# Prompt attention of a latent-attention layer: fifth score product with 128 rows, one rotary product for two heads, latent queries split after their norm

## Chip, core, metric

The kernel runs on one core of a Trainium2 chip (trn2). The metric is device time in microseconds of the whole program, on that core. A core has a tensor engine (PE, with PEld for its weight loads), a vector engine (DVE), a scalar engine (ACT), GpSimd (POOL) and SyncE (SP), which here only issues transfers; each takes its own instructions in order and they wait for each other by semaphores.

## What is computed

One step of a two-layer decoder trunk on 1024 prompt tokens and 8 sample tokens (1032 columns): a gated linear recurrence with its feed-forward block, then multi-head latent attention (MLA) with another. The change lies in the prompt's part of MLA. There are 8 heads, latents of 256 features, rotary keys of 64, queries from 384 latent features:

```python
q = (rmsnorm(h @ w_dq, q_a_norm) @ w_uq).reshape(B, T, H_B, NOPE + ROPE_DIM)   # 128 + 64
q_nope, q_rope = q[..., :NOPE], rope(q[..., NOPE:], pos)
...
s = (jnp.einsum('bthc,bsc->bhts', ql, c_all)
     + jnp.einsum('bthr,bsr->bhts', qr, kr_all)).astype(jnp.float32) * SCALE
s = jnp.where(k_pos <= q_pos, s, MASK_VALUE)
p = jax.nn.softmax(s, axis=-1)
return jnp.einsum('bhts,bsc->bthc', p, c_all)
...
def rope(x, pos):    # halves of 32
    return jnp.concatenate([x1 * cos - x2 * sin, x2 * cos + x1 * sin], axis=-1)
```

For the prompt the kernel expands the keys and values of each head from the latents instead of absorbing the projection into the query.

## The kernel before, in words

Everything is kept transposed, features on the partitions and the 1032 tokens in the free dimension, cut in NS = 3 spans of W = 344. A float32 value x is held as two parts, hi (rounded to the tensor engine's one-pass float32 format, F32R) and lo = x - hi; `split` (lines 127 to 130) makes them, hi on ACT and lo on DVE or another engine, and `mm3` (lines 172 to 179) forms a product as three: hi hi, hi lo, lo hi.

**Entry of MLA**, `mla_in` (lines 1137 to 1240). Six 128-column products with x give the latents (`cf`), the rotary keys (`krt`) and the latent queries (`qa`, three chunks of 128). `keys(s)` normalises the latents of a span and rotates the keys: the rotary columns are projected twice, straight and with their halves swapped (`swapped`, line 1079), so that one product with the table `tab` and one addition give the rotation. The key goes to `krs` (its hi part, on rows 0 to 63 and again on 64 to 127) and `krl` (its lo part, 64 rows). `queries(s)` splits `qa` of a span at once, then forms its norm; since the split queries are not normalised, the factor is kept in `rqs` and, times the table, in `rtab`.

**Prompt attention**, `mla_prompt`. `prep(h)` is a generator that projects one head in steps: two for its keys (`kh`, `kl`), then for each span one step for the 128 plain query columns (product, times `rqs`, split: hi on ACT, lo on POOL) and one for the rotary ones (128 columns: 64 straight and 64 swapped; times `rtab` on DVE, a copy of the lower half on ACT, an addition, then hi on rows 0 to 63 and lo on rows 64 to 127 of `qrs`). An even head also makes the values of itself and the next head, four steps. So a head has 8 steps, an even one 12.

`scores(h, i)` takes 128 queries (row block i of 8) against the keys up to them, in pieces of 256 to 512 columns (`PIECES`, 12 pieces for the 8 row blocks). A piece is a sum of five products in one PSUM bank:

```python
nc.tensor.matmul(out, lhsT=qrs[:, ts], rhs=krs[:, ks], start=False, stop=False)         # line 1341
last = n == len(pcs) - 1
nc.tensor.matmul(out, lhsT=qrs[0:ROPE, ts], rhs=krl[:, ks], start=False, stop=not last)  # line 1343
```

Lines 1338 to 1340 are the three of the latent part, 1341 is (hi, lo) against the hi keys with 128 rows, 1343 hi against the lo keys with 64 rows. The last piece of a row block gets the causal mask by a bfloat16 product (line 1346). Then DVE takes the maximum (1347), ACT the exponentials (1356), DVE scales (1361). `turn` transposes the weights on PE (1377) two row blocks later (LAG), `pv` multiplies with the values.

**Order.** `attend()` yields after each row block of each head; the loop at its end emits, after row block i of head h, the steps of `prep(h + 1)` that are due: `n = 8 + (4 if (h + 1) % 2 == 0 else 0)` spread over the 8 row blocks. After head 7 the place of `prep` is taken by the first work of the sample tokens (`sample_first`). From these the framework builds the order of each engine with a model of its own, `schedule_with_timeline_sim=True`; PSUM tiles come from a ring of 8 banks.

Of the kernel before, what the change touches and what calls it, by code (L numbers as in the profile page):

```python
# [8 lines left out]
F32 = mybir.dt.float32  # L9
F32R = mybir.dt.float32r  # L10
# [27 lines left out]
class Core:  # L38
    """Pools, constants and the pieces that every sub-layer shares."""
# [37 lines left out]
    def first_x(self, x_prompt):  # L77
        """Loads the first span of the input, in tiles of 128 tokens, a tile a step."""
# [28 lines left out]
    def load_gains(self, rows, among):  # L107
        """rows: (AP [n, 128]) list, transposed into one column per row. among: other loads' steps."""
# [18 lines left out]
    def split(self, hi, lo, src, lo_eng=None):  # L127
        """src = hi + lo exactly, both in the one-pass format."""
# [3 lines left out]
    def weight(self, src, a, b, gain=None, pool=None, nb=2, place=None, eng=None):  # L132
        """Loads [128, a, b] of a weight, times gain[:, a], as hi and lo parts."""
# [38 lines left out]
    def mm3(self, out, terms, first=True, last=True):  # L172
        """Sum of stationary^T moving over terms of ((wh, wl), (ah, al))."""
# [10 lines left out]
    def xproduct(self, wt, s, n=None):  # L184
        """A weight's product with a span of x; n: its number among the next sub-layer's first weights."""
# [27 lines left out]
    def put_x(self, s, c, y, gain):  # L213
        """x[s] chunk c = y * gain, as hi and lo parts."""
# [13 lines left out]
class Squares:  # L228
    """Sum of the squares of the KC chunks of a span. Four chunks at a time are summed over their
    partitions in the four column groups of the tensor engine."""  # L230
# [5 lines left out]
    def add(self, src, eng=None, place=None):  # L236
        """src: the next chunks of the span."""
# [27 lines left out]
def result(gen):  # L265
    """Runs a generator to its end; what it returns."""
# [7 lines left out]
# Order in which steps of neighbouring parts are emitted, for each sub-layer and part.  # L274
# [252 lines left out]
def ffn_first(w_in):  # L527
    """The first weights that ffn asks for."""
# [4 lines left out]
def ffn(k, w_in, w_out, r, end):  # L533
    nc, tc = k.nc, k.tc
    w_in = w_in.rearrange("(c p) f -> p c f", p=P)
    with ExitStack() as st:
# [6 lines left out]
        def inp(f):  # L543
            """The gated products of 128 of the features, a span a step."""
# [55 lines left out]
class OutProj:  # L600
    """acc[s] = w_out^T o, with o read back from DRAM into the tiles of x, which get the new x of a
    span when its products are done. The first span goes head by head, as weights arrive."""
# [16 lines left out]
    def first(self, n, heads=H - 1):  # L619
        """The first n heads' part of the first span, kept in the place of the last span."""  # L620
# [74 lines left out]
class HgrnGates:  # L695
    """Per-feature constants of the forget gate from the lower bounds, one column per head."""
# [30 lines left out]
def hgrn(k, c, w_in, gnorm, lbl, state, load, st_p, st_s, o_dram, v_dram, out):  # L727
    """Gated recurrence, one head at a time, in chunks of 128 tokens.

    Scores inside a chunk are split by the largest power of two that separates the two tokens:  # L730
    for each, both sides are scaled by their decay to a token between them, so that no exponent
    is positive. Distances from 32 up fill their own blocks of A; the shorter ones stay in the
    four 32-token blocks on the diagonal and are picked by a mask."""
# [7 lines left out]
    with ExitStack() as st:  # L741
# [22 lines left out]
        def proj(h):  # L764
            """Projections of one head, one span of one of them a step: f, q, i, g."""
# [89 lines left out]
        def gate(h, sig):  # L855
            """gnorm * g * sigmoid(g), in place of g."""
# [233 lines left out]
def swapped(src, lo):  # L1090
    """Sources of 64 rotary columns followed by the same with their halves swapped."""
# [810 lines left out]
```

## Time and profile before

| | us |
|---|---|
| device time, three runs | 3000.06, 3000.13, 2996.25; median 3000.06 |
| span of the profiled execution, first to last instruction | 2994.8 |
| PE busy | 2848.2 (95%) |
| DVE busy | 1787.6 (60%) |
| ACT busy | 1084.2 (36%) |
| POOL busy | 1014.8 (34%) |
| last work chain, share of the span by engine | PE 75%, DVE 15%, ACT 4%, issue 4%, POOL 1%, DMA 1% |
| MLA's entry | about 1560 to 1645 |
| prompt attention | 1645 to 1955 |
| sample attention, later half | 1955 to 2107 |

The time of the profiled execution itself is given by its span alone; the lowest of the three runs is 1.5 us above it and the median 5.3 us. Times of the trace count from the start of the span. A matmul's row has its start and a modelled end; matmuls overlap, so what one costs is read from start to start. "Idle before" and an arrow name what an engine waited for; L1343 is line 1343.

### The profile page before, as it was taken

The numbers are of one execution on the slowest core, as the hardware profiler recorded it, in microseconds if no ns is written. First come the engines' busy times: TensorE is split into PE (matmuls) and PEld (weight loads), VectorE is DVE, ScalarE is ACT, GpSimd is POOL, SyncE is SP. The second block draws the span as 40 slices with busy tenths as digits, with TensorE's granted clock in tenths as the row PEclk, the third lists the DMA queues.
The fourth block names the chain that finished last, engine by engine and source line by source line (L and its number), as shares of the span: only waits on it lengthen the run. The fifth ranks groups of instructions, "written<-read, shape, count | busy, mean of one in ns | idle before, by whom it ended". The sixth has DMA issues, their size and how long they took to land.

```text
span 2994.8 us, 54870 instructions
## 1 busy us (share of the span) xinstructions
PE 2848.2 (95%) x22468; PEld 2648.1 (88%) x22468; DVE 1787.6 (60%) x3526; ACT 1084.2 (36%) x2216; POOL 1014.8 (34%) x936
## 2 busy tenths in 40 slices
PE   7899889899999999999999999978999999999998
PEld 7888888888899999999878888845879999999998
DVE  8888888873444454444377777786353445444445
ACT  6555555555511111111255555533443111111112
POOL 3455455453422333223241111253134233322330
PEclk9999999999999999999999999989999999999999
DMA  5122222153311111111141111477432111111112
GB/s 180 52 65 64 66 63 63 59 190 100 116 50 43 48 48 48 49 43 50 29 128 51 39 47 50 143 294 272 135 105 66 43 49 48 48 49 43 50 47 103
DMA packets 237084, 242.26 MB, mean 81 GB/s; under 512 B 25443, under 2 KB 217489, under 8 KB 230817
## 3 DMA queue, kind: packets, MB, share of 16 engines
q1 hardware_dynamic: 211568, 169.87, 18.8%
q0 software_dynamic: 7456, 43.00, 3.9%
q10 hardware_dynamic: 17808, 25.89, 2.4%
q8 instruction: 177, 2.90, 0.4%
q14 instruction: 75, 0.61, 0.1%
HBM read 194.60 MB, written 44.12 MB: 80 GB/s over the span
## 4 chain that ended last, share of the span: by engine, by line
PE 75%; DVE 15%; ACT 4%; issue 4%; POOL 1%; DMA 1%; DVEq 0%; ACTq 0%; SPq 0%; POOLq 0%
PE ps L177 22%; PE ps L178 21%; PE ps L179 21%; PE ps L1450 2%; PE ps L252 2%; DVE X L878 1%; DVE E L875 1%; PE ps L1343 1%; DVE E L874 1%; PE ps L1377 1%; PE ps L1338 1%; DVE qe L927 1%; ACT sig L830 1%; DVE b L826 1%; DVE turned L1450 1%
## 5 line engine op out<-in xcount | busy, mean ns | idle before, releaser
L177 PE MATMUL ps<-xh,w 128*128 128x344 f32 x3360 | 1106.8, 330 | 1.7 <-ACT xh L221 1.7
L178 PE MATMUL ps<-xl,w 128*128 128x344 f32 x3360 | 1086.3, 323 | 1.7 <-DVE xl L222 1.7
L179 PE MATMUL ps<-xh,w 128*128 128x344 f32 x3360 | 1081.6, 322 | 0.0
L155 POOL TENSOR_TENSOR w<-raw,w 128x512 fp32r<-128x512 f32 (+1 forms) x360 | 468.1, 1321 | 794.4 <-ACT w L151 773.3
L177 PEld LDWEIGHTS ps<-xh,w 128*128 128x128 f32 x3360 | 641.3, 191 | 24.5 <-issue 10.9
L178 PEld LDWEIGHTS ps<-xl,w 128*128 128x128 f32 x3360 | 640.7, 191 | 15.3 <-issue 8.8
L179 PEld LDWEIGHTS ps<-xh,w 128*128 128x128 f32 x3360 | 640.1, 191 | 6.0 <-issue 5.6
L582 DVE TENSOR_TENSOR acc<-ps,acc 128x344 f32<-128x344 f32 x864 | 397.6, 514 | 0.0
L151 ACT CAST w<-raw 128x1024 fp32r<-128x1024 f32 (+3 forms) x206 | 207.6, 1008 | 423.8 <-PE ps L179 322.6
L177 PE MATMUL ps<-gh,w 128*128 128x344 f32 x1056 | 339.5, 323 | 0.5 <-ACT gh L129 0.3
L179 PE MATMUL ps<-gh,w 128*128 128x344 f32 x1056 | 339.1, 321 | 0.0
L178 PE MATMUL ps<-gl,w 128*128 128x344 f32 x1056 | 338.7, 321 | 0.0
L557 POOL TENSOR_TENSOR u<-u,a 128x344 f32<-128x344 f32 x132 | 122.2, 927 | 533.1 <-DVE u L556 528.5
L556 DVE TENSOR_TENSOR u<-ps,r 128x344 f32<-128x344 f32 x132 | 68.1, 516 | 388.6 <-PE ps L179 388.3
L129 ACT CAST gh<-u 128x344 fp32r<-128x344 f32 x132 | 63.5, 481 | 503.9 <-POOL u L557 503.9
L552 DVE TENSOR_TENSOR a<-ps,r 128x344 f32<-128x344 f32 x132 | 68.1, 516 | 233.1 <-PE ps L179 227.0
L177 PEld LDWEIGHTS ps<-gh,w 128*128 128x128 f32 x1056 | 198.7, 189 | 5.3 <-issue 1.7
L178 PEld LDWEIGHTS ps<-gl,w 128*128 128x128 f32 x1056 | 199.2, 189 | 1.1 <-DVE gl L130 0.8
L179 PEld LDWEIGHTS ps<-gh,w 128*128 128x128 f32 x1056 | 199.1, 189 | 1.1 <-issue 1.1
L130 DVE TENSOR_TENSOR gl<-u,gh 128x344 fp32r<-128x344 f32 x132 | 70.1, 531 | 150.5 <-ACT gh L129 150.5
L553 ACT ACTIVATE a<-a 128x344 f32<-128x344 f32 x132 | 64.5, 490 | 224.0 <-DVE a L552 223.8
L877 POOL TENSOR_TENSOR X<-lin,E 128x256 f32<-128x256 f32 x112 | 108.8, 976 | 79.2 <-ACT E L876 50.4
(373 smaller groups left out, 4178.6 us busy)
## 6 DMA issues: line engine op xcount, KB each, us to landing
raw<-in_w_ffn_in_dram SPq DMA_DIRECT2D x88, 512.0 KB
raw<-in_w_ffn_out_dram SPq DMA_DIRECT2D x44, 512.0 KB
raw<-in_w_in_a_dram SPq DMA_DIRECT2D x32, 512.0 KB
xs<-x_d SPq DMA_DIRECT2D x72, 172.0 KB
x_d<-acc ACTq DMA_DIRECT2D x9, 1376.0 KB
x_d<-y SPq DMA_DIRECT2D x3, 1376.0 KB
od_a<-oh ACTq DMA_DIRECT2D x24, 172.0 KB
od_a<-ol ACTq DMA_DIRECT2D x24, 172.0 KB
```

The source lines that it names most:

```text
L130: (lo_eng or self.nc.vector).tensor_tensor(out=lo, in0=src, in1=hi, op=ALU.subtract)
L151: nc.scalar.copy(wh[:, :n], raw[:, :n])
L155: eng.tensor_tensor(out=wl[:, sl], in0=raw[:, sl], in1=wh[:, sl], op=ALU.subtract)
L177: nc.tensor.matmul(out, lhsT=wh, rhs=ah, start=first and i == 0, stop=False)
L178: nc.tensor.matmul(out, lhsT=wh, rhs=al, start=False, stop=False)
L179: nc.tensor.matmul(out, lhsT=wl, rhs=ah, start=False, stop=last and i == n - 1)
L552: nc.vector.tensor_tensor(out=a, in0=pg, in1=r[s], op=ALU.mult)
L556: nc.vector.tensor_tensor(out=u, in0=pu, in1=r[s], op=ALU.mult)
L557: nc.gpsimd.tensor_tensor(out=u, in0=u, in1=a, op=ALU.mult)
L582: nc.vector.tensor_tensor(out=acc[s][:, dc, :], in0=po, in1=acc[s][:, dc, :], op=ALU.add)
L877: nc.gpsimd.tensor_tensor(out=Xl[:, :, 0, :], in0=kl[:, :, 0, :], in1=El[:, :, 0, :], op=ALU.mult)
L1450: return lambda *a, **kw: self.tc.keep_in_program_order(getattr(self.eng, name)(*a, **kw))
```

## The change

- `krl` gets 128 rows, the lo key twice, and the fifth product takes all 128 rows of `qrs`: hi and lo against the lo keys.
- An even head's `prep` projects the plain rotary columns of itself and the next head side by side (64 + 64 columns). The rotation takes the swapped halves by four copies of 32 rows on ACT out of PSUM (`sw`), two products with full tables `rcos` and `rsin`, an addition, and two splits of 64 rows. An odd head has no rotary product. The odd head's rotary query (`qr1`) has lo on top and hi below, two buffers. An odd head has 5 steps, an even one 12.
- `queries(s)` forms the norm first, multiplies `qa` by it and by SCALE, and splits after that; so the plain query needs no factor: hi and lo straight from PSUM, lo on DVE.
- `rqs` and `rtab` are gone; `rcos` and `rsin`, same size, are loaded by two more transfers of 128 x 1032 on SP. Small tiles move to `k.rp` (tags r0, r1).

The diff, without docstrings and the renaming of arguments:

```diff
-            krs, krl = krp[:, 0], krp[0:ROPE, 1]
+            krs, krl = krp[:, 0], krp[:, 1]
-            rqs = qp.tile([P, T], F32, name="rqs")
-            rtab = qp.tile([P, T], F32, name="rtab")
+            rcos, rsin = (qp.tile([P, T], F32, name=n) for n in ("rcos", "rsin"))
...
-        nc.sync.dma_start(out=tab, in_=c["rope"])
+        for n, t in enumerate((tab, rcos, rsin)):
+            nc.sync.dma_start(out=t, in_=c["rope"][n])
...
-            nc.scalar.copy(kr[:, sl], krt[ROPE:P, sl])
-            nc.vector.tensor_tensor(out=kr[:, sl], in0=kr[:, sl], in1=krt[0:ROPE, sl], op=ALU.add)
+            kt = ip.tile([ROPE, W], F32, name="kt", tag="nat", bufs=2)
+            nc.scalar.copy(kt, krt[ROPE:P, sl])
+            nc.vector.tensor_tensor(out=kr[:, sl], in0=kr[:, sl], in1=kt, op=ALU.add)
...
-            nc.vector.tensor_tensor(out=krl[:, sl], in0=kr[:, sl], in1=krs[0:ROPE, sl], op=ALU.subtract)
+            for rows in (slice(0, ROPE), slice(ROPE, P)):
+                nc.vector.tensor_tensor(out=krl[rows, sl], in0=kr[:, sl], in1=krs[0:ROPE, sl], op=ALU.subtract)
...
+            rq = yield from norm(qa, 3, s)
+            nc.vector.scalar_tensor_tensor(out=qa[:, :, sl], in0=qa[:, :, sl], scalar=SCALE, in1=rq.unsqueeze(1).to_broadcast([P, 3, W]), op0=ALU.mult, op1=ALU.mult)
             k.split(qah[:, :, sl], qal[:, :, sl], qa[:, :, sl])
-            rq = yield from norm(qa, 3, s)
-            nc.scalar.mul(out=rqs[:, sl], in_=rq, mul=SCALE)
-            nc.vector.tensor_tensor(out=rtab[:, sl], in0=rqs[:, sl], in1=tab[:, sl], op=ALU.mult)
...
+            two = h % 2 == 0
+            cols = [(slice(0, P), w_uq[:, :, w0:w0 + P])]
+            if two:
+                cols += [(slice(P + i * ROPE, P + (i + 1) * ROPE), w_uq[:, :, w0 + i * 192 + P:w0 + (i + 1) * 192]) for i in range(2)]
+            wt = k.weight(cols, 3, 256 if two else P, g_q)
...
+            if two:
+                rot[h] = qk[:, 2 * SEQ + 2 * T:]
+                rot[h + 1] = ap.tile([P, T], F32R, name="qr1", bufs=2)
...
-                qf = ap.tile([P, W], F32, name="qf", bufs=1)
-                nc.vector.tensor_tensor(out=qf, in0=pp, in1=rqs[:, sl], op=ALU.mult)
-                k.split(qh[:, sl], ql[:, sl], qf, nc.gpsimd)
+                k.split(qh[:, sl], ql[:, sl], pp)
...
                 yield
+                if not two:
+                    continue
...
-                rt = ap.tile([P, W], F32, name="rt", bufs=1)
-                nc.vector.tensor_tensor(out=rt, in0=pp, in1=rtab[:, sl], op=ALU.mult)
-                qr = ap.tile([ROPE, W], F32, name="qr", bufs=1)
-                nc.scalar.copy(qr, rt[ROPE:P, :])
-                nc.vector.tensor_tensor(out=qr, in0=qr, in1=rt[0:ROPE, :], op=ALU.add)
-                nc.scalar.copy(qrs[0:ROPE, sl], qr)
-                nc.vector.tensor_tensor(out=qrs[ROPE:P, sl], in0=qr, in1=qrs[0:ROPE, sl], op=ALU.subtract)
+                sw = k.rp.tile([P, W], F32, name="sw", tag="r0")
+                for i in range(4):
+                    nc.scalar.copy(sw[32 * i:32 * i + 32, :], pp[32 * (i ^ 1):32 * (i ^ 1) + 32, :])
+                qr = k.rp.tile([P, W], F32, name="qr", tag="r1")
+                nc.vector.tensor_tensor(out=qr, in0=pp, in1=rcos[:, sl], op=ALU.mult)
+                nc.vector.tensor_tensor(out=sw, in0=sw, in1=rsin[:, sl], op=ALU.mult)
+                nc.vector.tensor_tensor(out=qr, in0=qr, in1=sw, op=ALU.add)
+                for u, (hi, lo) in enumerate(((slice(0, ROPE), slice(ROPE, P)), (slice(ROPE, P), slice(0, ROPE)))):
+                    nc.scalar.copy(rot[h + u][hi, sl], qr[hi, :])
+                    nc.vector.tensor_tensor(out=rot[h + u][lo, sl], in0=qr[hi, :], in1=rot[h + u][hi, sl], op=ALU.subtract)
...
-                nc.tensor.matmul(out, lhsT=qrs[0:ROPE, ts], rhs=krl[:, ks], start=False, stop=not last)
+                nc.tensor.matmul(out, lhsT=qrs[:, ts], rhs=krl[:, ks], start=False, stop=not last)
...
-            n = 8 + (4 if (h + 1) % 2 == 0 else 0)
+            n = 5 + (7 if (h + 1) % 2 == 0 else 0)
```

How the built order moves, at three places. On PE, behind row block 2 of head 0 while head 1 is prepared (`ident,Pt` is a transpose of the weights, `qah` and `qal` the split latent queries, `krp` the rotary keys, `qk` a head's keys and queries), before:

```order
L1346 LDWEIGHTS identb
L1346 MATMUL ps<-negm,identb 128x128
L1377 MATMUL ps<-ident,Pt 128x128
L177 MATMUL ps<-qah,w 128x344
L178 MATMUL ps<-qal,w 128x344
L179 MATMUL ps<-qah,w 128x344
L177 MATMUL ps<-qah,w 128x344
L178 MATMUL ps<-qal,w 128x344
L179 MATMUL ps<-qah,w 128x344
L177 MATMUL ps<-qah,w 128x344
L178 MATMUL ps<-qal,w 128x344
L179 MATMUL ps<-qah,w 128x344
L1338 MATMUL ps<-qk 128x512
```

and with the change:

```order
L1355 MATMUL ps<-negm,identb 128x128
L1386 MATMUL ps<-ident,Pt 128x128
L1347 MATMUL ps<-qk 128x512
L1348 MATMUL ps<-qk 128x512
L1349 MATMUL ps<-qk 128x512
L1350 MATMUL ps<-krp,qk 128x512
L1352 MATMUL ps<-krp,qk 128x512
```

The nine matmuls of the odd head's rotary product are gone from between two row blocks; the fifth score product stays where it was (line 1352 of the changed kernel).

On DVE, the first rotary span of head 4 while head 3 is attended (`mx` is the maximum, `Pt` the weights, `ol` and `PTl` lo parts), before:

```order
L1301 TENSOR_TENSOR rt<-ps,rtab 128x344
L1360 RECIPROCAL rs<-sm 128x1
L1361 TENSOR_SCALAR Pt<-Pt,rs 128x384
L1304 TENSOR_TENSOR qr<-qr,rt 64x344
L1306 TENSOR_TENSOR qk<-qr,qk 64x344
L130 TENSOR_TENSOR ol<-ps,oh 128x256
L1295 TENSOR_TENSOR qf<-ps,rqs 128x344
L1347 TENSOR_REDUCE mx<-ps 128x1
```

and with the change:

```order
L1311 TENSOR_TENSOR qr<-ps,rcos 128x344
L1312 TENSOR_TENSOR sw<-sw,rsin 128x344
L1313 TENSOR_TENSOR qr<-qr,sw 128x344
L130 TENSOR_TENSOR ol<-ps,oh 128x256
L1316 TENSOR_TENSOR qk<-qr,qk 64x344
L1316 TENSOR_TENSOR qr_18448<-qr,qr_18448 64x344
L130 TENSOR_TENSOR qk<-ps,qk 128x344
L1356 TENSOR_REDUCE mx<-ps 128x1
```

Between a scaling of the weights and the next maximum there are now five rotary operations instead of three, and the plain query's lo part stands where its multiplication stood. This comes in every second head only.

On ACT, at MLA's entry, the queries of the last span (`sqm` are the squares for the norm, `nat` the latents on their way to the results), before:

```order
L206 ACTIVATE rs_q<-rs_y 128x344
L1190 ACTIVATE rqs<-rs_y 128x344
L151 CAST w<-raw 128x512
L1205 COPY nat<-ps 128x320 x2
L129 CAST qah<-qa 128x3x344
L1163 ACTIVATE sqm<-qa 128x1032
L1205 COPY nat<-ps 128x320 x2
```

and with the change:

```order
L205 ACTIVATE rs_y<-ps,eps 128x344
L206 ACTIVATE rs_q<-rs_y 128x344
L151 CAST w<-raw 128x512
L1205 COPY nat<-ps 128x320 x2
L1162 ACTIVATE sqm<-qa 128x1032
L129 CAST qah<-qa 128x3x344
L1205 COPY nat<-ps 128x320 x2
```

The squares no longer stand behind a split of the same span; the split that follows them is that of the span before, and the last span's comes after its norm.

## Rows read from the trace of the kernel before

**Rows 1.** The page: busy time, share of the span, instructions

```profile
PE 2848.2 (95%) x22468; PEld 2648.1 (88%) x22468; DVE 1787.6 (60%) x3526; ACT 1084.2 (36%) x2216; POOL 1014.8 (34%) x936
```

**Rows 2.** Stretches: us; busy us of PE, PEld, DVE, ACT, POOL; PEclk, DMA, GB/s

```profile
1560.00:1600.00 40.00, 35.15 (x213) 33.36 (x212) 35.04 (x62) 20.62 (x39) 9.62 (x9) 1.00 0.21 72
1725.77:1764.73 38.96, 38.96 (x239) 32.37 (x237) 30.43 (x79) 22.09 (x57) 7.65 (x14) 1.00 0.15 44
1764.73:1806.59 41.86, 41.86 (x274) 35.79 (x273) 31.48 (x81) 21.45 (x55) 6.63 (x13) 1.00 0.15 44
1940.00:1950.00 10.00, 10.00 (x62) 7.53 (x61) 7.12 (x22) 5.26 (x16) 2.09 (x3) 1.00 0.08 28
```

**Rows 3.** Timeline of PE, row block 5 of head 0: start us, us

```profile
1660.96 0.40 PE L1340 MATMUL ps<-qk 128*128 128x512 f32 x1
1661.19 0.40 PE L1341 MATMUL ps<-krp,qk 128*128 128x512 f32 x1
1661.52 0.49 PE L1343 MATMUL ps<-krp,qk 64*128 64x512 f32 x1
1661.94 0.39 PE L1338 MATMUL ps<-qk 128*128 128x256 f32 x1
1662.17 0.28 PE L1339 MATMUL ps<-qk 128*128 128x256 f32 x1
1662.29 0.28 PE L1340 MATMUL ps<-qk 128*128 128x256 f32 x1
...
1662.61 0.38 PE L1343 MATMUL ps<-krp,qk 64*128 64x256 f32 x1
1662.93 0.23 PE L1346 MATMUL ps<-negm,identb 128*128 128x128 bf16 x1
1662.99 0.61 PE L1377 MATMUL ps<-ident,Pt 128*128 128x128 f32 x4
```

**Rows 4.** Instructions on tile krp: min/median/max ns, first and last start

```profile
L1341 PEld LDWEIGHTS ps<-krp,qk x96: 187/188/192, 1645.3 to 1947.2; 128*128 128x128 f32 x96
...
L1343 PEld LDWEIGHTS ps<-krp,qk x96: 182/183/185, 1645.7 to 1947.7; 64*128 64x128 f32 x96
L1343 PE MATMUL ps<-krp,qk x96: 378/437/498, 1645.7 to 1947.7; 64*128 64x512 f32 x40, 64*128 64x256 f32 x32, 64*128 64x384 f32 x24
```

**Rows 5.** Timeline of PE, one product of nine matmuls, then the next scores

```profile
1669.60 0.32 PE L177 MATMUL ps<-qah,w 128*128 128x344 f32 x1
...
1671.02 0.39 PE L1338 MATMUL ps<-qk 128*128 128x512 f32 x1
```

**Rows 6.** Groups on DVE and ACT, 1725 to 1807: busy us, mean ns

```profile
L1301 DVE TENSOR_TENSOR rt<-ps,rtab 128x344 f32<-128x344 f32 x6 | 3.1, 514 | 1.6 <-PE ps L179 1.5
...
L1303 ACT COPY qr<-rt 64x344 f32<-64x344 f32 x6 | 2.9, 478 | 2.3 <-DVE rt L1301 1.6 <-DVE rs L1360 0.6
```

**Rows 7.** Timeline of DVE, then of PE: a row block scaled, then transposed

```profile
1783.25 1.30 DVE L1361 TENSOR_SCALAR Pt<-Pt,rs 128x640 f32<-128x640 f32 x1
...
1790.28 0.72 PE L1377 MATMUL ps<-ident,Pt 128*128 128x128 f32 x5
```

**Rows 8.** Timeline of ACT, DVE and PE at MLA's entry, last span of queries

```profile
1621.73 1.06 ACT L129 CAST qah<-qa 128x1032 fp32r<-128x1032 f32 x1
1622.69 1.06 ACT L1163 ACTIVATE sqm<-qa 128x1032 f32<-128x1032 f32 x1
...
1622.82 1.37 DVE L130 TENSOR_TENSOR qal<-qa,qah 128x1032 fp32r<-128x1032 f32 x1 [2.62 <-ACT qah L129]
...
1628.52 0.52 DVE L209 SCALAR_TENSOR_TENSOR rs_y<-rs_q,rs_y 128x344 f32<-128x344 f32 x1
...
1625.39 0.82 PE L198 MATMUL ps<-sqm,one 128*128 128x344 f32 x2 [2.43 <-DVE sqm L1165]
1625.79 0.79 PE L177 MATMUL ps<-ch,w 128*128 128x512 f32 x1
...
1630.39 0.33 PE L177 MATMUL ps<-qah,w 128*128 128x344 f32 x1
```

More of the change, by code (lines that the diff above doesn't have):

```diff
@@ L1121, in mla @@
             krp = qp.tile([P, 2, T], F32R, name="krp")
-            krs, krl = krp[:, 0], krp[0:ROPE, 1]
+            krs, krl = krp[:, 0], krp[:, 1]
             qah = qp.tile([P, 3, T], F32R, name="qah")
             qal = qp.tile([P, 3, T], F32R, name="qal")
-            rqs = qp.tile([P, T], F32, name="rqs")
-            rtab = qp.tile([P, T], F32, name="rtab")
-            mla_in(k, c, a, o, g_in, g_kv, g_c, r, ch, cl, krs, krl, qah, qal, rqs, rtab, cns, krn, cnat)
+            rcos, rsin = (qp.tile([P, T], F32, name=n) for n in ("rcos", "rsin"))
+            mla_in(k, c, a, o, g_in, g_kv, g_c, r, ch, cl, krs, krl, qah, qal, rcos, rsin, cns, krn, cnat)
             x_done()
@@ L1132, in mla, with mla_in @@
                 nc.gpsimd.memset(SA, -1e30)
-                mla_prompt(k, ep, c, a, w_ukv, g_q, ch, cl, krs, krl, qah, qal, rqs, rtab, qns, qrn, o_dram, pages, lambda pool: sample_first(k, w_ukv, pages, qp, ep, pool, qns, QS))
+                mla_prompt(k, ep, c, a, w_ukv, g_q, ch, cl, krs, krl, qah, qal, rcos, rsin, qns, qrn, o_dram, pages, lambda pool: sample_first(k, w_ukv, pages, qp, ep, pool, qns, QS))
                 mla_sample(k, c, w_ukv, pages, qp, pick, SA, cns, krn, cnat, qrn, QS, o_dram, later, fill)
-def mla_in(k, c, a, o, g_in, g_kv, g_c, r, ch, cl, krs, krl, qah, qal, rqs, rtab, cns, krn, cnat):
+def mla_in(k, c, a, o, g_in, g_kv, g_c, r, ch, cl, krs, krl, qah, qal, rcos, rsin, cns, krn, cnat):
     nc, tc = k.nc, k.tc
@@ L1143, in mla_in @@
         tab = ip.tile([P, T], F32, name="tab")
-        nc.sync.dma_start(out=tab, in_=c["rope"])
+        for n, t in enumerate((tab, rcos, rsin)):
+            nc.sync.dma_start(out=t, in_=c["rope"][n])
         cf = ip.tile([P, 2, T], F32, name="cf")
-        kr = ip.tile([ROPE, T], F32, name="kr")
         qa = ip.tile([P, 3, T], F32, name="qa")
@@ L1253, in weave, with mla_prompt @@
             pass
-def mla_prompt(k, ep, c, a, w_ukv, g_q, ch, cl, krs, krl, qah, qal, rqs, rtab, qns, qrn, o_dram, pages, first):
+def mla_prompt(k, ep, c, a, w_ukv, g_q, ch, cl, krs, krl, qah, qal, rcos, rsin, qns, qrn, o_dram, pages, first):
     nc, tc = k.nc, k.tc
@@ L1266, in mla_prompt @@
         negm = vp.tile([P, P], BF16, name="negm", bufs=1)
-        negw = ap.tile([P, P], F32, name="negw", tag="qf", bufs=1)
+        negw = k.rp.tile([P, P], F32, name="negw", tag="r0")
         nc.sync.dma_start(out=negw, in_=c["negmask"])
         nc.vector.tensor_copy(negm, negw)
-        pair = {}
-        ready = {}
+        pair, ready, rot = {}, {}, {}
         def prep(h):
             w0 = h * 192
-            wt = k.weight(
-                [(slice(0, P), w_uq[:, :, w0:w0 + P])] + [(slice(P + d.start, P + d.stop), x) for d, x in swapped(w_uq, w0 + P)],
-                3, 256, g_q)
+            two = h % 2 == 0
[3 more added lines that the diff above has]
+            wt = k.weight(cols, 3, 256 if two else P, g_q)
             wk = k.weight(w_ukv[:, :, h * 256:h * 256 + P], 2, P)
-            qk = (ep, ap)[h % 2].tile([P, QK], F32R, name="qk", tag=f"qk{h % 2}", bufs=1)
+            qk = (ep, ap)[h % 2].tile([P, QK + (T if two else 0)], F32R, name="qk", tag=f"qk{h % 2}", bufs=1)
             kh, kl = (qk[:, i * SEQ:(i + 1) * SEQ] for i in range(2))
-            qh, ql, qrs = (qk[:, 2 * SEQ + i * T:2 * SEQ + (i + 1) * T] for i in range(3))
+            qh, ql = (qk[:, 2 * SEQ + i * T:2 * SEQ + (i + 1) * T] for i in range(2))
+            if two:
+                rot[h] = qk[:, 2 * SEQ + 2 * T:]
+                rot[h + 1] = ap.tile([P, T], F32R, name="qr1", bufs=2)
             for hf in range(2):
@@ new lines, in prep @@
+                nc.vector.tensor_tensor(out=qr, in0=pp, in1=rcos[:, sl], op=ALU.mult)
[4 more added lines that the diff above has]
+                    nc.vector.tensor_tensor(out=rot[h + u][lo, sl], in0=qr[hi, :], in1=rot[h + u][hi, sl], op=ALU.subtract)
+                    if s == NS - 1:
+                        nc.scalar.copy(qrn[:, h + u, :], qr[hi, W - NB:])
@@ L1310, in prep @@
                 yield
-            ready[h] = (qh, ql, qrs, kh, kl)
+            ready[h] = (qh, ql, rot[h], kh, kl)
             if h % 2 == 0:
@@ L1530 @@
 FB = (LAT + ROPE) // M
-QK = 2 * SEQ + 3 * T
+QK = 2 * SEQ + 2 * T
 EARLY = KN['early']
@@ L1545, in sample_first @@
         if n % 2 == 0:
-            pages.ropes(n, (old, ("rqs", "rtab")[n // 2], 1))
+            pages.ropes(n, (old, ("rsin", "rcos")[n // 2], 1))
     for n in (4, 5, 6):
@@ L1559, in sample_first @@
             next(turns, None)
-        wkt = pool.tile([P, 256], F32, name="wkt", tag=("qf", "rt")[h % 2], bufs=1)
+        wkt = k.rp.tile([P, 256], F32, name="wkt", tag=f"r{h % 2}")
         nc.scalar.copy(wkt, pt[:, :256])
@@ L1602, in mla_sample @@
         frees = [8 * (n // 4) + (14, 17)[n % 4 // 2] for n in range(4 * NB)]
-        ropes = [(old, "rqs", 1), (old, "rtab", 1)] + [(k.wp, "raw", 2)] * 2
+        ropes = [(old, "rsin", 1), (old, "rcos", 1)] + [(k.wp, "raw", 2)] * 2
         owner = {j: j for j in range(8)}
@@ L1754, in mla_sample @@
                     next(fill, None)
-        wr = up_half(k, w_ukv, 1, [place([P, 1024], "wu", (old, t, 1)) for t in ("rtab", "rqs")])
+        wr = up_half(k, w_ukv, 1, [place([P, 1024], "wu", (old, t, 1)) for t in ("rcos", "rsin")])
         pf = k.psum()
@@ L1852, in constants @@
     cos, sin = np.cos(ang), np.sin(ang)
-    rope = np.concatenate([cos, cos, -sin, sin]).astype(np.float32)
+    rope = np.stack([np.concatenate(r) for r in ([cos, cos, -sin, sin], [cos] * 4, [-sin, sin] * 2)]).astype(np.float32)
     negmask = np.where(t[None, :] > t[:, None], -1e30, 0.0).astype(np.float32)
```

6 lines of the change are left out of this document (3 added, 3 removed).

## Prediction

> **What bounds the kernel now.** I read the page first: PE is busy for 95% of the span, DVE for 60% [rows 1]. That is an average over stages, so next comes the view of stretches, cut where the last transposition of a head stands, two row blocks into the next head [rows 2]. The first long stretch is head 2 attended while head 3 is prepared, the second head 3 attended while head 4 is prepared. PE is busy for all of both (38.96 of 38.96, 41.86 of 41.86), DVE for 30.43 and 31.48 (78% and 75%), ACT for about half. So in the prompt's attention PE sets the pace, and whatever leaves PE's queue shortens the stage, until DVE is full. Since PE has no gap there, a busy sum says nothing of what one product costs; I take that from start to start in PE's timeline [rows 3, 5].
>
> **Fifth score product.** A product of 512 columns with 128 rows takes 0.23 us from start to start (1660.96 to 1661.19). The 64-row one starts 0.33 after the product before it and holds PE for 0.42 until the next [rows 3]: 0.10 + 0.19 = 0.29 us more than a plain product. The next product, 256 wide, then takes 0.23 (1661.94 to 1662.17) where its neighbour takes 0.12: 0.11 more. In the same row block's last piece, 256 wide and followed by the bfloat16 mask product, the 64-row product holds PE for 0.32 against 0.12. The modelled durations of the 64-row form are long too, 378 to 498 ns, and there are 96 of them [rows 4]: 64 at the end of a row block, 32 with another piece behind them. The stationary operand of line 1341 is the same tile with 128 rows, and that product runs at 0.23; so I expect the changed line to run as 1341 does. Sum: 96 x 0.29 = 27.8, and 32 x 0.11 = 3.5 for the follower, 31.3 at the most. What no row shows is a 128-row product with the mask product behind it: the step to bfloat16 could itself cost the 0.20 that I gave to the 64 rows, 64 x 0.20 = 12.8, so 18.5 at the least. The excess is nearly the same whether the mask follows (0.20) or a float32 product (0.19), and the mask's own follower starts 0.06 behind it, with no wait at the step back [rows 3]. That is nearest to the upper end; I take **28**.
>
> The weight load of the 64-row product lasts 183 ns, that of the 128-row one 187 or 188 [rows 4]: the load is not longer or shorter, it comes later. The Trainium skill (TensorE: Matmul & The Clock Gate, LDWEIGHTS) says that a load's time depends on its columns and not on its rows; taken alone, that rule leaves 64 rows nothing to cost, this part would give 0 and the whole sum would be 17. The trace agrees on the load and speaks against the 0, by the 0.29 above; it is the first rival. Another page of the Trainium skill (TensorEngine Tiling, Key Properties) says that a change of the array's tiling mode drains it; if 64 rows count as another mode, that is the late load of the rows.
>
> **Rotary products.** Four odd heads lose three products of nine matmuls. One takes 1.42 us (1669.60 to 1671.02) [rows 5]: 12 x 1.42 = **17.0**. They stand between row blocks with PE full, so this is path. The 12 products of the even heads stay as wide as before.
>
> **DVE and ACT in the attention.** The stretch of head 2 holds four plain and three rotary spans, that of head 3 two and three. At 0.51 us for 344 columns [rows 6], taken for 64 rows and for all-SBUF operands too: head 2's stretch loses 4 multiplications and 3 x 3 rotary operations (6.6), gains 4 subtractions that POOL did (2.0), 30.4 - 6.6 + 2.0 = 25.8 us, in 38.96 - 12 x 0.29 - 3 x 1.42 = 31.2 us of PE: 83%. Head 3's stretch loses 2 and 9 (5.6), gains 2 and 3 x 5 (8.7), 34.6 us in 41.86 - 3.5 = 38.4: 90%. ACT loses two copies of 0.48 [rows 6] per rotary span and gains six: 21.5 - 2.9 + 8.6 = 27.2 us of 38.4. So DVE comes near PE in every second stretch without passing it. What keeps a queue that is 90% full from holding PE is the lead: row block 4 of head 3 is scaled by 1784.55 and transposed at 1790.28, 5.7 us later [rows 7]. I charge 2 us over the stage for moments when the lead runs out; it could be 0, and 8 if each of the three stretches with an even head's preparation stalls for 2 to 3. The weights of odd heads get a third smaller on every engine; that is hidden and left out. The moved small tiles and the PSUM bank that four copies now hold (4 x 0.48 = 1.9 us) are paid for by the same lead and the ring of eight banks; they are part of the 8.
>
> **MLA's entry.** The split of the last span's queries used to run ahead of its squares on ACT, 1.06 us [rows 8]; PE stood still for 2.43 us waiting for those squares (start 1625.39), and behind the gap twelve key products took 1625.79 to 1630.39, 4.6 us, where at 0.23 each they would take 2.8. With the squares first the gap should shrink by up to 1.06. Against it, the last span's split now ends a chain: from 1625.39 the norm takes until 1629.04, 3.65 us, then one multiplication and one subtraction of 1032 columns on DVE (at most 1.37 each, the subtraction's row) and the cast, 1.06: 7.45 us. PE has 5.0 us to the first query product and 4 x 1.42 of the first two spans before it needs them: 10.7, or 8.8 if the key products run at 0.23 (1625.39 to 1625.79, then 2.8). So it is covered, by 1.3 us at the worst. DVE, with 35.0 of 40 us busy at the start of the entry [rows 2], gets three more 64-row subtractions, at most 1.5 us; DMA is at 0.21 there, and the two added tables (0.53 MB each) have nothing to wait for but earlier transfers. I book the entry at 0, with -3 (gap and slow products gone) and +4 (DVE late, the split late) as ends.
>
> **Behind the prompt.** Nothing is reordered after it. The sample attention's first gathers are long under way when head 7 ends: DMA is at 0.08 from 1940 to 1950 [rows 2], so a shorter head 7 collides with nothing; if it did, the 3.5 us of that head (12 x 0.29) would be given back.
>
> **Sum.** -17 - 28 + 2 + 0 = -43 on the profiled execution, 2994.8 to 2951.8 us of span. The median of the runs stands 5.3 above that span, the lowest 1.5. From the median, 3000.1 - 43 = **2957**. Ends: -31.3 - 17 - 3 = -51 gives 2949, or 2946 measured against the lowest run; -18.5 - 17 + 8 + 4 = -24 gives 2976. The range is 2946 to 2976.
>
> **Rivals.**
> First, what is slow is not the 64 rows but the place, the last product of a sum; then the fifth product gains nothing and the time is 3000 - 17 = 2983. For it: the equal weight loads. Against it: lines 1341 and 1343 have the same stationary tile and width, the load of 1343 starts late before anything of the next sum is in play, and they differ in rows. 0.06. (The Trainium skill's rule on LDWEIGHTS, above, is on this side.)
> Second, DVE becomes the bound in the stretches that prepare an even head. Then those three keep their old length and give back 3 x 3.5, and the 2 become 4 with the waits around them: about 2969. For it: 90%, in order, five operations in a row ahead of a maximum. Against it: the lead, and that the stretches between have room. 0.17; its time lies in the range.
> Third, on the other side: the rotary step itself stops PE. Its PSUM tile waits for ACT four times, behind exponentials; if the ring of eight banks has no other bank free, PE stands for the chain of 1.9 + 3 x 0.51 = 3.4 us, and what runs behind a stop can run slow, as the twelve products at the entry did (1.8 more). Nine such steps in the attention cost 9 x 5.2 = 47, more than the 45 gained: about 3002 to 3004. It decides from the point where all nine stop in full; one in two would still leave a gain of 20. Against it: PE is busy for the whole of both stretches today [rows 2], with twice as many rotary steps, though each holds its bank for less. 0.04.
> Fourth, a mixture of losses that I do not see leaves less than 17: 0.04, half of it within the resolution.
>
> **Chances.** The forecast (2946 to 2966) has 0.69, the second rival 0.17; together 0.86 within the range. Differences under 0.2%, 6 us, can hardly be told from none here. Faster by more: the forecast, both rivals that only shrink it, half of the mixture, 0.94; same 0.02; slower 0.04.
>
> **What would show it.** Right: the product of line 1352 starts 0.23 behind 1350 at 512 columns and its follower 0.23 behind it; `qah` matmuls of 344 columns fall by 108; the stretches of heads 2 and 3 become 31 and 38 to 39 us with PE still full, DVE at about 83% and 90%. Wrong: PE idle behind `PTh` or `Pt` in the stretches with an even head's preparation, a mask product that still starts 0.3 us late, or PE idle behind `qal` at the entry.

## The result, and the profile after

| | before | changed |
|---|---|---|
| median of 4 runs each, same chip, us | 2999.22 (2996.25 to 3000.13) | 2951.74 (2947.82 to 2952.82) |
| profiled execution, span, us | 2994.8 | 2949.3 |

The ratio is 0.9847, 95% interval 0.9833 to 0.9861: 46 us less, 42 to 50. Predicted were 43 less and 2957.

The page of the changed kernel; busy time, share of the span, instructions:

```profile
PE 2806.7 (95%) x22360; PEld 2635.9 (89%) x22360; DVE 1770.6 (60%) x3505; ACT 1091.2 (37%) x2245; POOL 993.0 (34%) x912
```

Against [rows 1], 108 matmuls are gone and no share has moved by more than a point; the page says nothing of where the time went. The two stretches of [rows 2] do (head 2 attended while head 3 is prepared, then head 3 while head 4 is; columns as there):

```profile
1718.76:1749.65 30.89, 30.89 (x211) 28.11 (x210) 24.51 (x69) 18.41 (x51) 4.43 (x11) 1.00 0.15 46
1749.65:1787.75 38.10, 38.10 (x274) 35.88 (x273) 32.67 (x85) 26.91 (x69) 4.00 (x10) 1.00 0.16 49
```

38.96 became 30.89 and 41.86 became 38.10; PE is full in both, DVE at 79% and 86%. Row block 5 of head 0 in PE's timeline (start, duration), against [rows 3]:

```profile
1663.34 0.39 PE L1350 MATMUL ps<-krp,qk 128*128 128x512 f32 x1
1663.57 0.39 PE L1352 MATMUL ps<-krp,qk 128*128 128x512 f32 x1
1663.81 0.28 PE L1347 MATMUL ps<-qk 128*128 128x256 f32 x1
1663.92 0.28 PE L1348 MATMUL ps<-qk 128*128 128x256 f32 x1
```

The fifth product (L1352) starts 0.23 behind the fourth, holds PE for 0.24, and its follower is held 0.11, no longer 0.23. In row block 4 the mask comes 0.12 behind the fifth product of 256 columns and the transposition 0.06 behind the mask:

```profile
1660.01 0.28 PE L1352 MATMUL ps<-krp,qk 128*128 128x256 f32 x1
1660.13 0.23 PE L1355 MATMUL ps<-negm,identb 128*128 128x128 bf16 x1
1660.19 0.50 PE L1386 MATMUL ps<-ident,Pt 128*128 128x128 f32 x3
```

MLA's entry, against [rows 8] (PE's timeline: the last norm's product, the first of the twelve key products, the first query product):

```profile
1626.09 0.82 PE L198 MATMUL ps<-sqm,one 128*128 128x344 f32 x2 [0.80 <-ACT nat L1205]
1626.48 0.66 PE L177 MATMUL ps<-ch,w 128*128 128x512 f32 x1
...
1629.53 0.33 PE L177 MATMUL ps<-qah,w 128*128 128x344 f32 x1
```

The gap of 2.43 us is 0.80, and the twelve key products take 3.05 instead of 4.60. What they no longer pay is the clock: behind the gap of the kernel before, the granted clock was at its lower level (0.50, which is 1.2 of 2.4 GHz) for 3.41 us; in the changed kernel it is at 1.00 throughout (the view of stretches, before and changed):

```profile
1626.15:1629.56 3.41, 3.41 (x10) 2.64 (x9) 1.04 (x2) 2.00 (x5) 0.00 (x0) 0.50 0.34 106
```
```profile
1626.48:1629.53 3.05, 3.05 (x15) 2.42 (x13) 1.14 (x3) 2.23 (x5) 0.00 (x0) 1.00 0.39 120
```

But a stop that the kernel before did not have stands ahead of the first transposition of attention, and behind it the granted clock is at half (the timeline of PE, then the view of stretches):

```profile
1652.93 0.47 PE L1386 MATMUL ps<-ident,Pt 128*128 128x128 f32 x1 [3.39 <-DVE nm L1361]
```
```profile
1652.93:1658.48 5.55, 5.55 (x19) 4.74 (x19) 3.23 (x11) 2.23 (x8) 0.83 (x1) 0.50 0.15 35
```

I follow the difference by one event a stage: the first key product (1625.79 before, 1626.48 after), the eight transpositions that close head 0 (1683.91, 1680.63), the last weighted sum of the prompt (1954.43, 1912.96), and the final products of the sample stage (2107.53, 2061.66). The transpositions and the final products are taken from the chain that ended last; PE's timeline begins their rows 0.16 earlier. Entry to key products +0.7; head 0 58.12 to 54.15, -4.0; heads 1 to 7 -38.2; sample stage -4.4. Together -45.9 of the span's -45.5.

### The profile page after: what moved, and what is told of

It reads as the page before. It is cut to its first block, busy times and chain, and to the rows that moved or that the text cites. A ratio compares the mean times of both kernels' runs of the same rounds, so it can differ in the third digit from the quotient of the medians.

```text
span 2949.3 us, 54597 instructions
## 1 busy us (share of the span) xinstructions
PE 2806.7 (95%) x22360; PEld 2635.9 (89%) x22360; DVE 1770.6 (60%) x3505; ACT 1091.2 (37%) x2245; POOL 993.0 (34%) x912
## 4 chain that ended last, share of the span: by engine, by line
PE 75%; DVE 14%; ACT 5%; issue 4%; POOL 1%; DMA 1%; SPq 0%; DVEq 0%; ACTq 0%; POOLq 0%
PE ps L177 22%; PE ps L178 22%; PE ps L179 22%; PE ps L252 2%; PE ps L1459 1%; DVE E L875 1%; DVE X L878 1%; PE ps L1386 1%; DVE E L874 1%; DVE turned L1459 1%; DVE b L826 1%; PE ps L198 1%; DVE qe L927 1%; ACT sig L830 1%; ACT w L151 1%
## 5 line engine op out<-in xcount | busy, mean ns | idle before, releaser
L151 ACT CAST w<-raw 128x1024 fp32r<-128x1024 f32 (+4 forms) x206 | 206.2, 1002 | 425.3 <-PE ps L179 325.1
L877 POOL TENSOR_TENSOR X<-lin,E 128x256 f32<-128x256 f32 x112 | 108.9, 977 | 79.2 <-ACT E L876 48.4
```

The lines of the kernel that those rows point to most:

```text
L151: nc.scalar.copy(wh[:, :n], raw[:, :n])
L877: nc.gpsimd.tensor_tensor(out=Xl[:, :, 0, :], in0=kl[:, :, 0, :], in1=El[:, :, 0, :], op=ALU.mult)
```

## Experiments

The runs below were on four chips. On two of them the kernel before takes 3012 us, on the other two 2997 to 2998; so every time is read as a ratio to the kernel before on its own chip, and its us are this ratio on a kernel of 2999. "The attention" is the time from the first key product to the last weighted sum, 328.6 us in the kernel before.

**The fifth product alone, and its counterpart.** The kernel before with

```
-krs, krl = krp[:, 0], krp[0:ROPE, 1]
+krs, krl = krp[:, 0], krp[:, 1]        # and krl written on both halves
-matmul(out, lhsT=qrs[0:ROPE, ts], rhs=krl[:, ks], ...)
+matmul(out, lhsT=qrs[:, ts], rhs=krl[:, ks], ...)
```

> The kernel before with one part of the change alone: the fifth score product takes all 128 rows (krl on both halves of the partitions). Theory rows: a 64-row product among 128-row ones costs 0.29 to 0.33 us, whatever stands behind it; 96 of them, so 31 us less than the kernel before, about 2968 us, and the product of the fifth line 0.23 behind the fourth at 512 columns. Rival place: the last product of a sum is slow with any number of rows; then 2999 us, with the three added 64-row subtractions (1.5 us at most) hidden or on top.

Measured: 2981.33 against 3011.83, ratio 0.9903 (0.9883 to 0.9922), 29 us less (23 to 35). The same two stretches:

```profile
1719.78:1754.90 35.12, 35.12 (x238) 32.35 (x237) 30.21 (x79) 21.82 (x57) 8.27 (x14) 1.00 0.17 48
1754.90:1792.94 38.04, 38.04 (x275) 35.82 (x273) 31.01 (x81) 21.74 (x55) 6.66 (x13) 1.00 0.16 48
```

Each is 3.82 to 3.84 shorter than in [rows 2]: 12 products of 0.32. Eight such heads would make 30.6, but the whole attention lost 28.6 (300.07): heads 1 to 5 lost 3.83 each, while heads 6 and 7, attended beside the first work of the sample tokens, lost 3.5 and 1.7. The changed kernel with `lhsT=qrs[0:ROPE, ts], rhs=krl[0:ROPE, ks]`:

> The changed kernel with the fifth product back on 64 rows (rows 0 to 63; in odd heads these hold the low part of the queries, so there the product takes another operand than the reference's). Theory rows: 31 us more than the changed kernel, about 2983 us; what is left against the kernel before, 16 to 17 us, is then the rotary part, 12 products of 1.42. Rival place: 2952 us, and the rotary part would be worth all 47.

Measured: 0.9934 (0.9918 to 0.9951), 20 us less than the kernel before (15 to 25). Its stretches:

```profile
1723.23:1757.92 34.69, 34.69 (x212) 28.09 (x210) 25.05 (x69) 18.75 (x51) 4.19 (x11) 1.00 0.13 40
1757.92:1799.84 41.92, 41.92 (x274) 35.85 (x273) 32.99 (x85) 26.70 (x69) 3.77 (x10) 1.00 0.15 45
```

The first lost 4.27 of 38.96, three products of 1.42; the second, where an even head is prepared, nothing. The run is 26 us slower than the changed kernel (0.9934 against 0.9847), where I expected 31: the two stretches are longer by the 3.8 due to each, but at head 0 this run lost only 0.9, as its stop there is shorter (2.50 us instead of 3.39, told below) and the clock did not fall behind it. The two parts add up within their intervals (29 + 20 against 46), and the rival of the place falls.

**Where the 64 rows stand.** The kernel before, the line of the 64-row product moved to the front of the sum:

> The kernel before with its 64-row product put first in the sum instead of last; the last product before the mask is now a 128-row one. Theory rows: the excess moves with the 64 rows, 2999 us within 4, and the product behind the 64-row one starts 0.4 late at 512 columns. Rival place: the place at the end was slow, a plain product stands there now at 0.23, and 96 x 0.29 = 28 us go: about 2971 us.

Measured: 1.0029 (1.0020 to 1.0039), 9 us more (6 to 12). The place theory falls again, and my 2999 within 4 misses. PE's timeline:

```profile
1707.59 0.28 PE L1343 MATMUL ps<-krp,qk 128*128 128x256 f32 x1
1707.71 0.23 PE L1346 MATMUL ps<-negm,identb 128*128 128x128 bf16 x1
...
1709.54 0.28 PE L179 MATMUL ps<-w,cl 128*128 128x256 f32 x1
1709.75 0.49 PE L1339 MATMUL ps<-krp,qk 64*128 64x512 f32 x1
1710.17 0.50 PE L1340 MATMUL ps<-qk 128*128 128x512 f32 x1
1710.51 0.39 PE L1341 MATMUL ps<-qk 128*128 128x512 f32 x1
```

The 128-row product now ahead of the mask is quick (0.12). The 64-row one (L1339) starts 0.21 behind a product that takes 0.12, holds PE for 0.42, and its follower for 0.34. That follower's 0.11 was paid 32 times in the kernel before, where the short mask product took the place 64 times; now 96 times: 64 x 0.11 = 7 of the 9 us. The trace agrees: the attention takes 336.07, 7.4 more.

**Two 64-row products in a row.** The changed kernel with the fifth line on rows 0 to 63, twice:

> The changed kernel with the fifth product issued as two 64-row products in a row, both on rows 0 to 63 (so one half is counted twice and the other left out). A plain product takes 0.18 us on average over the widths. Theory switch: only the step from 128 rows to 64 and back costs, 31 us once, and the second product adds 96 x 0.18 = 17: about 3000 us. Theory each: every 64-row product is late by 0.29, so the second adds 96 x 0.47 = 45: about 3028 us.

Measured: 0.9988 (0.9979 to 0.9998); against the run with one such product (0.9934), 16 us more; the attention takes 330.02 against 312.72, 17.3 more. Predicted by the switch theory were 17, by the other 45. PE's timeline:

```profile
1702.50 0.39 PE L1350 MATMUL ps<-krp,qr 128*128 128x512 f32 x1
1702.82 0.49 PE L1352 MATMUL ps<-krp,qr 64*128 64x512 f32 x1
1703.16 0.38 PE L1353 MATMUL ps<-krp,qr 64*128 64x512 f32 x1
1703.47 0.39 PE L1347 MATMUL ps<-qk 128*128 128x256 f32 x1
```

0.32 + 0.34 + 0.31: the pair takes 0.65 where one took 0.42, 0.23 more, what a plain product takes. So the step in and the step out cost, not the product. The Trainium skill (TensorEngine Tiling (Array Packing), Key Properties) says that changing the tiling mode drains the engine, and changing the tile alone does not. The trace fits this, if 64 rows count as another mode, at a price of 0.29 to 0.4 us for in and out; how much of it is a drain and how much the late weight load, no row separates.

**The stop at head 0.** The changed kernel's own run, and three edits of it. Early table: `preload_act_table_set("natural_log_exp_and_others")` on ACT after the mask's load. Filler: `while done * 8 < (i + 1 + (3 if h == 0 else 0)) * n`.

> The changed kernel itself, on the chip of the next three runs, so that they can be set against it: 0.9847 of the kernel before, and the same stop of PE of 3.4 us ahead of the first transposition of row block 0 of head 0, with the clock at half for some 5.5 us behind it.

> The changed kernel with the table of exponentials loaded at the start of the prompt part, in a moment in which ACT is idle, instead of ahead of the first exponential. Theory chain: the stop at head 0 is the wait for row block 0's scaled exponentials, and the table's 1.28 us lie on that chain; the stop falls from 3.4 to 2.1 us, and the time by 1.3 us, or by up to 4 if the clock no longer falls behind it. Rival theory, DVE: the chain is held by DVE's rotary work; the stop stays at 3.4 and the time too.

> The changed kernel with the products that prepare head 1 emitted earlier in head 0 (three more eighths of its five steps), so that 2 x 1.42 us of query products stand ahead of the first transposition. Theory chain: PE's stop shrinks by 2.8 less the casts of 0.45 that these products put into ACT's queue ahead of the exponentials: to 1 or 1.5 us, and the time by 2 to 5 us with the clock. Rival theory: later row blocks of head 0 lack the products that were taken from between them, and PE stops there; the time stays within 1 us.

> Both edits together. Theory chain: no stop at head 0 beyond some tenths of a us and no fall of the clock, 3.4 + 2.8 = 6.2 us less than the changed kernel, a fifth of a per cent. Rival theory, as above: stops elsewhere in head 0 take it back.

Then five of head 0's six 64-row subtractions on POOL (`eng = nc.gpsimd if h == 0 and (u, s) != (0, 0) else nc.vector`), with and without the filler:

> The table early and the earlier products as in the run before this, and in head 0 five of the six 64-row subtractions of the rotary queries on POOL, which is idle there, instead of DVE: 5 x 0.51 = 2.6 us less in DVE's queue. Theory DVE: what is left of the stop, 2.24 us ahead of the transpositions of row block 1, is DVE's queue; it falls to some tenths of a us, and head 0 ends 7 us earlier than in the changed kernel (5.3 with the two edits alone), the clock staying at full. Rival theory, ports: POOL's operations (0.93 us for one of 128 x 344 in the kernel before) stretch the DVE operations beside them, and the stop stays at 2 us.

> The table early and the five subtractions on POOL, without the earlier products. Theory DVE: the stop of 2.83 us (with the table early alone) ends when row block 0 is scaled; four of the five subtractions and their 2.0 us stood ahead of it, so 0.8 to 1.5 us of stop are left, the clock stays at full, and head 0 ends 4 to 5 us earlier than in the changed kernel. Rival theory, ACT: the casts and swap copies on ACT hold the chain; the stop stays above 2.3 us.

Head 0 is the time from the first key product to its last transpositions, 58.12 us in the kernel before; the clock is the granted one behind the stops:

| run | stops of PE at its start, us | clock behind them | head 0, us | less the stops, us | ratio to before |
|---|---|---|---|---|---|
| changed kernel, again | 3.39 | 0.50 for 5.7 us | 54.07 | 50.68 | 0.9841 (0.9827 to 0.9854) |
| early table | 2.83 | 0.50 for 3.4 us | 52.46 | 49.63 | 0.9830 (0.9817 to 0.9844) |
| filler | 0.94, 1.72 | 1.00 | 51.27 | 48.61 | 0.9834 (0.9821 to 0.9848) |
| both | 2.24 | 1.00 | 50.83 | 48.59 | 0.9833 (0.9819 to 0.9846) |
| both, and POOL | 0.97 | 1.00 | 49.44 | 48.47 | 0.9829 (0.9815 to 0.9842) |
| early table, and POOL | 2.44 | 0.50 for 3.4 us | 52.11 | 49.67 | 0.9837 (0.9824 to 0.9850) |

Without its stops head 0 takes 48.5 to 48.6 us wherever the clock stayed at full, 1.1 more where it was at half for 3.4 us, and 2.1 more where it was at half for 5.7. In head 0 each helps; over the whole run the differences, 1 to 5 us, are within the intervals. The early table took 0.56 from the stop, not 1.28, since both queues stand in the chain. In the changed kernel the first exponential waited for ACT, which copied, cast and loaded the table up to 1650.25, and the scaling behind it then waited for other work of DVE until 1652.61 (the timelines of ACT and DVE):

```profile
1648.97 1.28 ACT L1365 ACT_TABLE_LOAD   x1
1650.27 0.37 ACT L1365 ACTIVATE Pt<-ps,nm 128x128 f32<-128x128 f32 x1
```
```profile
1652.61 0.27 DVE L1370 TENSOR_SCALAR Pt<-Pt,rs 128x128 f32<-128x128 f32 x1
```

With the early table the exponential begins at 1646.93 and the scaling at 1650.00: what ACT gave up, DVE's queue took in part. With both edits no 6.2 us came back but 3.2, since the stop moved one row block on, where DVE is still behind (the timelines of both edits, and with POOL):

```profile
1653.69 0.44 PE L1387 MATMUL ps<-ident,Pt 128*128 128x128 f32 x2 [2.24 <-DVE Pt L1371]
```
```profile
1654.23 0.44 PE L1388 MATMUL ps<-ident,Pt 128*128 128x128 f32 x2 [0.97 <-DVE Pt L1372]
```

POOL relieves DVE by less than the 2.6 us taken off it: head 0 gains 1.4 with the filler and 0.35 without, and both forecasts miss. With the filler I expected head 0 to end 7 us earlier than in the changed kernel, and it ends 4.7 earlier. Without it I expected a stop of 0.8 to 1.5, and 2.44 lies where the rival, ACT, put it; but there the exponential begins only 0.26 behind its maximum (1647.35 to 1647.61), and its scaling stands 2.2 in DVE's queue (1648.07 to 1650.24), so the rival's number does not show its cause. Of the run with both edits and POOL, DVE and POOL side by side:

```profile
1645.58 2.32 DVE L155 TENSOR_TENSOR w<-raw,w 128x512 fp32r<-128x512 f32 x2
...
1650.76 0.83 DVE L1372 TENSOR_SCALAR Pt<-Pt,rs 128x128 f32<-128x128 f32 x1
```
```profile
1645.37 0.92 POOL L1318 TENSOR_TENSOR qk<-qr,qk 64x344 fp32r<-64x344 f32 x1 [3.88 <-ACT qk L1316]
1646.36 1.26 POOL L1318 TENSOR_TENSOR qr<-qr,qr 64x344 fp32r<-64x344 f32 x1
...
1650.58 0.93 POOL L1318 TENSOR_TENSOR qk<-qr,qk 64x344 fp32r<-64x344 f32 x1
```

The two weight subtractions take 2.32 us beside POOL's, 1.01 in the changed kernel with POOL idle; the scaling of 128 columns 0.83, not 0.27. The Trainium skill (SBUF — State Buffer, SBUF: two separate sides) says that GpSimd and a DVE instruction in a fast mode or with two SBUF inputs lock each other out of a port pair; DVE's rows agree.

**Value products later.** As the run with POOL and filler, and `fill0 = prep(0)` run for nine steps only, its last three put ahead of head 1's:

> The table early, the five subtractions on POOL, and now head 0's value products (12 of 256 columns in each of four steps, 1.4 us a step) put behind row block 0's scores for three of the four steps, as further cover for the chain of the first exponentials; their splits on ACT and DVE then come behind that chain too. Theory DVE: the stop of 0.97 us that was left goes, the clock stays at full, and from the first key product to the end of head 0 it takes 48.2 to 48.7 us (54.15 in the changed kernel, 49.44 with the filler of query products); some 6 us less than the changed kernel in all. Rival theory: the same work of DVE is only moved, and the stop comes back a row block later; then 49.4 us or more.

Measured: 0.9849 (0.9836 to 0.9863), head 0 55.08, a stop of 4.13 us. The rival's time came true (49.4 or more), but neither mechanism: the stop is not later, but larger. Most value products landed between row block 0's third score product and its fourth (1639.24 and 1643.13), not behind its scores; and the swap copies of the third rotary step still stand on ACT ahead of the first exponential (copies to 1647.58, the exponential from 1648.95). The cover was used up and the chain stayed.

**How near DVE is to the bound.** Behind the sum in a rotary step, three times `tensor_tensor(out=sw, in0=sw, in1=rsin[:, sl], op=mult)`:

> The changed kernel with three more multiplications of 128 x 344 on DVE in each rotary step (their results replace a tile that nothing reads any more). In a stretch that prepares an even head that is 9 x 0.43 to 0.51 = 3.9 to 4.6 us more, 36.3 to 37.0 of 38.1 us, 95 to 97%. Theory pace: the stretches keep 38.1 us, since PE sets their pace until DVE is full, and only head 0 gets longer, by 3 to 5 us, where DVE is already the bound. Rival theory, DVE as the bound: at over 90% the lead is gone; the three stretches get longer by 1 us or more each.

Measured: 0.9854 (0.9839 to 0.9869), within the intervals of the changed kernel; heads 1 to 7 together take 235.0 instead of 232.3. Two such stretches, and one of PE's stops in the first:

```profile
1679.68:1718.81 39.13, 38.52 (x274) 36.00 (x273) 36.22 (x94) 26.50 (x69) 3.81 (x10) 1.00 0.17 51
1749.70:1788.83 39.13, 38.49 (x274) 36.01 (x273) 36.17 (x94) 26.50 (x69) 3.77 (x10) 1.00 0.16 48
```
```profile
1710.90 0.85 PE L1388 MATMUL ps<-ident,Pt 128*128 128x128 f32 x6 [0.61 <-DVE sm L1369]
```

38.1 became 39.1 with 36.2 us of DVE, 93%: the rival was right about the load, and the changed kernel lies less than these 3.5 to 3.8 us of DVE short of it. Head 0, against my expectation, did not get longer (53.49): its one stop became several short ones (0.89, 1.36, 0.34, 2.16), behind which the clock stayed at full. Nine operations cost DVE 3.5 to 3.8 us of busy time, about 0.4 each, though each lasts 0.51.

## Why the prediction was right, point by point

**What bounds the kernel.** Right: PE is full in the stretches and what left its queue left the time.

**Fifth score product, 28: the mechanism was right, and that the size came so near is in part luck.** In heads 1 to 5 it is 3.83 each, 30.6 for eight such heads; the attention of the run with this part alone lost 28.6 (29, 23 to 35, by its ratio), since heads 6 and 7 lost less. I had held back 3 for a mask product that might itself cost 0.20 behind 128 rows; it starts 0.12 behind a product of 256 columns and costs nothing. What heads 6 and 7 did not give I had not thought of. I also had the sharing of the follower's 0.11 right, and did not use it for the place.

**Rotary products, 17.0: right.** With this part alone the stretches that prepare an odd head lost 4.27 (heads 2 and 4) and 4.1 (head 6), so 17 for four; 20 (15 to 25) by the ratio.

**DVE and ACT in the attention, +2 in the stretches: wrong in place and size.** The stretches that prepare an even head lost nothing: 38.10 against my 38.4, no stop. DVE was at 32.7 us, not 34.6. Each of the two stretches held three plain spans before, not four and two as I had counted, which leaves both sums as they were. What did not hold is 0.51 for every operation, read up to its end or to the start of the next. The 18 new ones took 8.3 us instead of 9.2, since the full-width ones begin 0.43 behind each other in a full queue; the 12 that went had taken 6.8 instead of 6.1, since one subtraction ran beside POOL's multiplication of weights (1772.11, 1.50 us). The smaller weights, which I had left out, took 0.5 less.

The 1.30 of row block 4's scaling [rows 7] was no plain duration either: POOL's query subtraction ran beside it, from 1783.27 for 0.94, and with that subtraction gone from POOL it takes 0.55. But POOL's multiplication of weights, which slowed the subtraction before, now runs beside a scaling of 384 columns, which takes 1.96 us where it took 0.42 (DVE's timeline of the changed kernel, then POOL's):

```profile
1754.97 1.96 DVE L1370 TENSOR_SCALAR Pt<-Pt,rs 128x384 f32<-128x384 f32 x1
```
```profile
1754.97 1.47 POOL L150 TENSOR_TENSOR raw<-raw,gains 128x768 f32<-128x768 f32 x1 [7.02 <-DVE rs L1369]
```

So the scalings of that stretch took 0.6 us more, not less. Scalings of 640 and of 384 columns in the whole attention, by form, before and after:

```profile
L1361 DVE TENSOR_SCALAR Pt<-Pt,rs 128x640 f32<-128x640 f32 x8 | 7.1, 883 | 0.1
L1361 DVE TENSOR_SCALAR Pt<-Pt,rs 128x384 f32<-128x384 f32 x8 | 3.5, 440 | 0.3
```
```profile
L1370 DVE TENSOR_SCALAR Pt<-Pt,rs 128x384 f32<-128x384 f32 x8 | 6.2, 779 | 0.2
L1370 DVE TENSOR_SCALAR Pt<-Pt,rs 128x640 f32<-128x640 f32 x8 | 4.4, 545 | 0.0
```

The cost stood where I had charged nothing: in head 0, whose rotary steps run ahead of attention, not between finished row blocks. There PE has no lead of work, DVE and ACT are nearly full (8.04 and 8.96 of 9.40 us up to 1649.4), and the first exponentials and their scaling wait behind other work in both. By the products removed and the quicker key products head 0 should have lost 3.8 + 4.3 + 1.6 = 9.7; it lost 4.0. The 5.7 are the stop of 3.39 and some 2.2 for the half clock behind it. The runs bear this out: 58.12 less 9.7 is 48.4, and where the clock stayed at full, head 0 took 48.5 to 48.6 without its stops. The price is the third rival's, 3.4 and 1.8 for what runs slow, once instead of nine times; the mechanism is another, not the PSUM banks of a rotary step that I named there, but the queues of DVE and ACT ahead of the first exponentials. Of the end of 8 for this term, 5.7 were used.

**MLA's entry, 0: its parts reached their good end, the time did not.** The gap lost 1.6, where I had 1.06 at the most, and the key products 1.6, by the clock that no longer fell. But the key products start 0.7 later in this execution (between 1624.05 and 1626.48 in all runs with this entry), so the first query product comes only 0.9 earlier (1630.39, 1629.53). What came later ahead of them I did not trace.

**Behind the prompt, 0: 4.4 less, left open.** The last gather of rotary rows held DVE for 3.07 before and 0.82 after, which is half. From the last weighted sum to the final products it took 153.1 before and 148.7 after; on the chips on which the kernel before takes 2997 to 2998, four runs of the changed kernel with the edits above took 147.5 to 150.4. So 153.1 lies above all five, but it is one execution; and on the other two chips eight runs, two of them of the kernel before with an edit, took 161.6 to 167.5 without a difference between the kernels. A stage that varies by 6 us from run to run and by 15 from chip to chip does not let that one profile settle 4.

**The sum.** Against the 43 booked, the span shows 2.6 more in the fifth product, 1.6 in the key products and 4.4 behind the prompt; and 0.7 less at their start, 3.7 less at head 0 beyond the 2 booked, and 1.4 less in heads 1 to 7 (38.2, where 30.6 - 3.8 + 17.1 - 4.3 = 39.6 were due). Of these 0.9 are in head 6, whose last row block meets a stop of PE of 0.48 that the kernel before does not have (ahead of the transpositions at 1885.79, behind DVE's scaling). So 45.5 came out, with 0.4 more time in the rest of the program: the two large terms held, and the small errors cancelled in part. In my range one end was off by one: 51 off the lowest run, 2996.3, is 2945, not 2946.

## What to carry to other kernels

Where an engine is full, price its work from start to start; one short row dimension among full ones can cost more than the whole product it shortens. Price the start of a pipelined stage by itself: work that hides between finished steps later has no cover in the first one. Before moving work to a second engine, ask what the first does more slowly beside it, and what else then runs beside it.

## What the runs showed of the hardware beyond that

- 64-row products cost by the switch, 0.29 us in and out and 0.11 for a 128-row float32 product behind; a second one in a row costs only its own 0.23 (512 columns, granted clock 1.00).
- At head 0 the granted clock fell to the lower level (1.2 GHz, 0.50 over the 5.55 us shown) behind the stop of 3.39 us, and fell behind those of 2.44, 2.83 and 4.13; behind 2.24 and shorter ones it stayed at 1.00. The length of the stop alone does not decide: with the fifth product back on 64 rows it stayed at 1.00 behind a stop of 2.50, and at MLA's entry it fell behind stops of 2.43, 2.37 and 1.98 (the kernel before, and the two runs that edit it).
- Edits of some us at head 0 show in the trace of one execution, and not in the ratios of five runs (the same code gave head 0 54.15 and 54.07 us on two chips).
